# HGRN layer: VectorE's and ScalarE's instruction orders written by hand beside TensorE's, with weight splits and projection finishes at fixed places

## The chip, the cores and the metric

The kernel runs on one core of one Trainium2 chip. Its time is the device time of one execution in microseconds (us), and lower is better. Three executions of the kernel before were timed; a profiled execution of the same program gives the trace that is read below.

Five engines matter: TensorE (PE; its weight loads are shown apart as PEld), VectorE (DVE), ScalarE (ACT), GpSimd (POOL) and SyncE (SP), which issues the DMAs. Each takes its own instructions in their order, and semaphores tie the engines together.

## The reference: what is computed

A trunk of two layers over 512 tokens of width 1024, in float32. Each layer has a token mixer, a squared-ReLU MLP and a gated embedding, with a layer norm after mixer and MLP. Layer 0 mixes with Mamba-2 SSD, layer 1 with HGRN2, and the change touches the HGRN2 mixer alone:

```python
q, fz, v, g = jnp.split(u @ w_in, 4, axis=-1)
log_f = jnp.logaddexp(jnp.log(lb), jnp.log1p(-lb) + jax.nn.log_sigmoid(fz))
k = (1.0 - lb) * jax.nn.sigmoid(-fz)
...
b_cs = jnp.cumsum(chunked(log_f, k_dim), axis=2)
...
def step(s_prev, inp):
    q_, kk, v_, b_ = inp
    diff = b_[:, :, None] - b_[:, None, :]
    dec = jnp.exp(jnp.where(mask, diff, -jnp.inf))
    scores = jnp.einsum('blhk,bshk,blshk->bhls', q_, kk, dec)
    o = jnp.einsum('bhls,bshv->blhv', scores, v_) + jnp.einsum('blhk,bhkv->blhv', q_ * jnp.exp(b_), s_prev)
    b_last = b_[:, -1]
    s_new = jnp.exp(b_last)[..., None] * s_prev + jnp.einsum(
        'bshk,bshv->bhkv', kk * jnp.exp(b_last[:, None] - b_), v_)
    return s_new, o
...
o = rms_norm(o, norm_w).reshape(bsz, seq, D_MODEL) * jax.nn.silu(g.astype(jnp.float32))
return o.astype(u.dtype) @ w_out
```

There are 8 heads of 128 channels. A score between two tokens carries, for each of the 128 channels, the product of the forget gates between them.

## The kernel before, in words

**Products in float32.** A weight tile of 128x1024 comes by one DMA into a raw tile (three of them). A *split* makes two tiles of it: ACT casts it to the high part (`whi`, L113) and DVE subtracts that from the raw tile to get the low part (`wlo`, L115). Every product is then three matmuls (`mm3`, L119 to L121): high x high, high x low, low x high. Six buffers hold high parts and six low parts.

**The HGRN stage** has two strands that share TensorE.

The *background* computes projections that need no head's result: query and forget gate of a head (`qf`, two tiles, 16 `mm3`), values and gates of two heads (`vg`, four tiles), and the first half of the output projection (`out0`). They run in the order `q0 q1`, then `JOBS`: q2 q3 q4 q5 v2 q6 q7 v3 o (the values of heads 0 to 3 are computed ahead of the stage). A projection's *finish* empties its PSUM banks: for `qf` a copy (L880), a table load, a sigmoid (L882), a scaling (L883), a second sigmoid (L885) and a scaling (L886) on ACT; for `vg` four bank copies (L863) and a Silu over two tiles (L865).

The *core* (`hcore`) takes the heads in pairs: 0/1, 2/3, 4/5, 6/7. Scores within 32 tokens are built in levels m = 0 to 4. At the first, third and fifth level (m = 0, 2, 4) TensorE multiplies keys by queries for each block of 32 tokens (L981: 88, 56 and 16 columns), into one PSUM bank per head. DVE then multiplies keys and queries by decays (L987, L992) and the decays among themselves (L1000), once a level, and copies the scores out of the bank through masks (L962). `distant` (L955, L956) makes the queries of the next wide level. After the levels come blocks farther apart (L1046), transposes of the keys (L1077), state sums (L1089, L1093), outputs (L1107, L1109), a norm with the gate (L1114 to L1119) and transposes of the result (L1127), which ACT and DVE split (L1128, L1129). `enter_heads` (L935) prepares the next pair.

**What sets the order.** `hcore` is a generator: at each `yield n` the caller lets the background run for about n us of matmuls (`fill`), so TensorE's order is written out by hand (`manual_schedule` with TensorE alone). FILL, STEPS, AHEAD and LAST hold those amounts; for heads 6 and 7 they are scaled by 0.78. On VectorE, ScalarE and the DMA queue a scheduler orders the instructions by priority. In `unit` a split has a raised priority (LEAD = 100) and is placed as the scheduler sees fit; the finish of a projection is recorded directly behind its last matmul; `issue_after` ties `enter_heads` to a state copy (L1091).

The PSUM buffers: four banks for projections (`pj`), two for the cores' scores and outputs (`py0`, `py1`, one per head of the pair), one for transposes (`pt`), one for sums (`pm`). A new tile of a tag with one buffer waits until the last reader of the old one is done: the third level's matmuls wait for the masked copies of the first.

## Time and profile before

| what | value |
|---|---|
| runs timed | 1424.92, 1425.13, 1426.7 us (median 1425.13) |
| profiled execution, its own time | 1426.6 us |
| its span, first to last instruction | 1424.8 us |
| TensorE's granted clock over the span | 1.00 |
| VectorE / ScalarE busy in the stretch 820 to 1020 us | 142.3 / 115.9 us of 200 |
| HBM traffic over the span | 124 GB/s |

The profile is one execution of the program, taken by the hardware profiler. A row of the view in order of time has the start in us, the duration in us, the engine, the line of the kernel, the operation, "out<-in" with the tiles' names, the shapes, how many alike follow each other (x), and in brackets the idle time of the engine before it with what ended that. A row of the view by groups has the busy time, the mean duration in ns and the idle time before. TensorE's rows overlap, since matmuls are pipelined and their ends are modelled; its pace is read from the starts. Line numbers are those of the kernel before; after the change they are higher (old L962, L987, L1128 are new L1014, L1037, L1184).

### The profile page before, as it was taken

What the parts mean: (1) busy time and instruction counts of PE and PEld (TensorE: products, weight loads), DVE (VectorE), ACT (ScalarE), POOL (GpSimd) and SP (SyncE); (2) the same over time, 40 slices, a digit from 0 to 9 for tenths busy, and PEclk for the clock granted to TensorE, in tenths of its full rate; (3) what the DMA queues carried; (4) which work ended last, traced back from release to release, by engine and by line L of the source; (5) the groups of instructions that cost most, each with busy time, mean ns of one, the idle gap of its engine ahead of it and who ended that gap; (6) DMA issues with size and microseconds to landing.
All of it is one profiled execution on the core that took longest, in us unless ns stands there. A gap on an engine that the chain in (4) does not pass through costs nothing.

```text
span 1424.8 us, 20421 instructions
## 1 busy us (share of the span) xinstructions
PE 1413.6 (99%) x8061; PEld 1174.6 (82%) x8061; DVE 1057.4 (74%) x1760; ACT 754.5 (53%) x1134; POOL 1.8 (0%) x12
## 2 busy tenths in 40 slices
PE   9999999999999999999999999999999999999998
PEld 7888888888888888888888887887898888888887
DVE  7988687787967667677986576678685867667873
ACT  6776454563265454545545547655555454544641
POOL 0000000000000000000000000000000000000000
PEclk9999999999999999999999999999999999999999
DMA  8432323333433444444621321222163444444231
GB/s 298 142 130 92 119 89 119 104 107 126 152 119 121 158 130 153 133 148 163 215 82 49 133 90 60 75 90 90 50 232 104 148 137 145 148 133 163 89 118 45
DMA packets 49392, 178.02 MB, mean 125 GB/s; under 512 B 5521, under 2 KB 6289, under 8 KB 49169
## 3 DMA queue, kind: packets, MB, share of 16 engines
q1 hardware_dynamic: 49296, 176.73, 36.8%
q8 instruction: 63, 1.03, 0.3%
q14 instruction: 33, 0.26, 0.1%
HBM read 174.54 MB, written 2.16 MB: 124 GB/s over the span
## 4 chain that ended last, share of the span: by engine, by line
PE 94%; DVE 3%; ACT 2%; DMA 1%; issue 0%; SPq 0%; ACTq 0%; DVEq 0%
PE pj L119 23%; PE pj L120 23%; PE pj L121 23%; PE py L119 5%; PE py L121 5%; PE py L120 5%; PE py L735 1%; PE py L741 1%; PE py L981 1%; PE pm L705 1%; DVE wlo L115 1%; PE pt L233 1%; PE pt L693 1%; DMA r<-in_w 1%; PE py L1107 0%
## 5 line engine op out<-in xcount | busy, mean ns | idle before, releaser
L113 ACT CAST whi<-raw 128x1024 fp32r<-128x1024 f32 x222 | 233.0, 1052 | 330.3 <-PE pj L120 234.1
L119 PE MATMUL pj<-b,whi 128*128 128x512 f32 (+1 forms) x1006 | 382.1, 381 | 0.7 <-ACT b L237 0.7
L120 PE MATMUL pj<-b,whi 128*128 128x512 f32 (+1 forms) x1006 | 380.6, 379 | 1.0 <-DVE b L238 1.0
L121 PE MATMUL pj<-b,wlo 128*128 128x512 f32 (+1 forms) x1006 | 379.2, 377 | 0.0
L115 DVE TENSOR_TENSOR wlo<-raw,whi 128x1024 fp32r<-128x1024 f32 x222 | 269.8, 1220 | 142.2 <-ACT whi L113 136.8
L120 PEld LDWEIGHTS pj<-b,whi 128*128 128x128 f32 x1006 | 189.4, 188 | 34.2 <-DVE b L238 1.2
L119 PEld LDWEIGHTS pj<-b,whi 128*128 128x128 f32 x1006 | 188.9, 188 | 34.1 <-ACT b L237 0.9
L121 PEld LDWEIGHTS pj<-b,wlo 128*128 128x128 f32 x1006 | 189.2, 188 | 33.6
L121 PE MATMUL pj<-whi,b 128*128 128x512 f32 x544 | 212.8, 392 | 0.0
L119 PE MATMUL pj<-whi,b 128*128 128x512 f32 x536 | 212.7, 397 | 0.0
L120 PE MATMUL pj<-wlo,b 128*128 128x512 f32 x536 | 210.2, 393 | 0.0
L121 PEld LDWEIGHTS pj<-whi,b 128*128 128x128 f32 x544 | 102.1, 188 | 20.9
L119 PEld LDWEIGHTS pj<-whi,b 128*128 128x128 f32 x536 | 100.7, 188 | 20.6 <-ACT b L1128 0.6
L120 PEld LDWEIGHTS pj<-wlo,b 128*128 128x128 f32 x536 | 100.8, 188 | 19.4
L113 ACT CAST whi<-r 128x1024 fp32r<-128x1024 f32 x72 | 75.7, 1053 | 67.8 <-PE pj L121 38.6
L115 DVE TENSOR_TENSOR wlo<-r,whi 128x1024 fp32r<-128x1024 f32 x72 | 87.6, 1219 | 23.8 <-ACT whi L113 23.2
L121 PE MATMUL py<-whi,b 128*128 128x512 f32 (+1 forms) x250 | 96.9, 388 | 0.0
L120 PE MATMUL py<-wlo,b 128*128 128x512 f32 x224 | 87.2, 389 | 0.0
L119 PE MATMUL py<-whi,b 128*128 128x512 f32 x224 | 87.1, 390 | 0.0
L121 PEld LDWEIGHTS py<-whi,b 128*128 128x128 f32 x250 | 46.9, 188 | 9.7
L634 DVE SCALAR_TENSOR_TENSOR cv<-pj,cst,cv 128x509 f32<-128x509 f32 (+2 forms) x66 | 48.7, 744 | 3.6 <-ACT cv L631 2.8
L119 PEld LDWEIGHTS py<-whi,b 128*128 128x128 f32 x224 | 42.1, 188 | 9.1 <-DVE sg L494 0.3
(303 smaller groups left out, 1864.7 us busy)
## 6 DMA issues: line engine op xcount, KB each, us to landing
raw<-in_w SPq DMA_DIRECT2D x112, 512.0 KB, 3.3
r<-in_w SPq DMA_DIRECT2D x64, 512.0 KB, 3.4
raw<-in_wssd SPq DMA_DIRECT2D x36, 512.0 KB, 3.4
a<-csd SPq DMA_DIRECT2D x16, 512.0 KB, 3.6
raw<-in_wso SPq DMA_DIRECT2D x16, 512.0 KB, 3.3
raw<-in_wg SPq DMA_DIRECT2D x16, 512.0 KB, 3.4
raw<-in_whq SPq DMA_DIRECT2D x16, 512.0 KB, 3.3
raw<-in_whvg SPq DMA_DIRECT2D x14, 512.0 KB, 3.2
```

What stands on the lines that cost most here:

```text
L113: nc.scalar.copy(hi[:, :n], f)
L115: nc.vector.tensor_sub(lo[:, :n], f, f32(hi[:, :n]))
L119: nc.tensor.matmul(out, sh, mh, start=start, stop=False, **kw)
L120: nc.tensor.matmul(out, sh, ml, start=False, stop=False, **kw)
L121: nc.tensor.matmul(out, sl, mh, start=False, stop=stop, **kw)
L233: nc.tensor.transpose(pt[:, j * P : (j + 1) * P], src[:, k * P : (k + 1) * P], ident)
L634: nc.vector.scalar_tensor_tensor(cv[:, d:], ps[:, : T - d], convw[:, i, k : k + 1], cv[:, d:], ALU.mult, ALU.add)
L693: nc.tensor.transpose(pt[:, c * P : (c + 1) * P], xs[:, c * P : (c + 1) * P], ident)
L705: nc.tensor.matmul(pst_[:, c * P : (c + 1) * P], btok[:, c, :], xw[:, c].rearrange("p h q -> p (h q)"), start=True, stop=True)
L735: nc.tensor.matmul(yd[64 * r : 64 * r + 64, sl], xdt[:, 2 * c + r, :], m[:, r, sl], start=True, stop=True)
L741: nc.tensor.matmul(yo[:, c * P : (c + 1) * P], pv[:, c - 1].rearrange("p h q -> p (h q)"), cm[:, c * P : (c + 1) * P], start=True, stop=True,)
L981: nc.tensor.matmul(pcs[r][bs, at : at + n], kk[r][:, ts], qs, start=True, stop=True)
```

## The change

ScalarE and VectorE join `manual_schedule`: their instructions in the HGRN stage now stand in the order in which the source records them. What was left to the scheduler gets a place:

- **Loads and splits.** All weight tiles are listed ahead (`sources`). `lift` issues the next load; `feed` splits one raw tile if fewer than READY = 4 split tiles wait, and lifts another; `take` hands the background the oldest split tile. `feed` stands at the end of the levels' stages, after the state sums and after each transposition of results.
- **Finishes.** `qf` and `vg` put their finish into a list (`due`), and `flush` carries it out: at each stage's end, when the next `qf` begins (all but one), when `vg` takes its third bank, before `out0`, and when a core needs the result.
- **The core.** `distant` of the third level is recorded one level earlier, and the first and third levels' masked copies one level later, behind the products of the second and fourth. `enter_heads` runs `distant` of the first level, and is no longer tied to a state copy.

The core of the diff:

```diff
+READY = 4
+    def flush(n=0):
+        while len(due) > n:
+            due.pop(0)()
+    def feed(n=1):
+        while n and raised and len(ready) < READY:
+            ready.append(split(raised.pop(0), 0))
+            lift()
+            n -= 1
+    def take():
+        if not ready:
+            feed()
+        u = ready.pop(0)
+        if not cores:
+            feed()
+        return u
...
-                units.append(unit(a["whvg"][4 * i + j]))
+                units.append(take())
             if j == 0:
+                if c == 2:
+                    flush()
                 pss[c] = bank(psj, "pj")
...
     def qf(h):
+        flush(1)
...
-            hi, lo = unit(a["whq"][2 * h + w])
+            hi, lo = take()
...
+        due.append(finish)
...
             if m in wide:
                 pcs = [py(r) for r in R]
-                for r in R:
-                    distant(r, half)
...
-            for r in R:
+            if m == 1:
+                for r in R:
+                    distant(near[r], qd[r], tot[r], 4)
+            for r in R if m not in wide else ():
                 sc, scb, pc = scs[r], scbs[r], pcs[r]
-                if m in wide:
-                    n = 88 - wide[m]
-                    u = half
+                if m < 4:
+                    w = m - 1
+                    n = 88 - wide[w]
+                    u = 1 << w
...
             if m not in wide:
+                flush()
+                feed()
                 yield FILL[0] * STEPS[m // 2]
...
         if h0 < 6:
-            for r in R:
-                need("qf", h0 + 2 + r)
-            with tc.issue_after(carried.ins):
-                enter_heads(h0 + 2)
+            enter_heads(h0 + 2)
+        feed()
...
             nc.vector.scalar_tensor_tensor(s.l(i0 + r), pt, hnw[:, 0:1], f32(s.h(i0 + r)), ALU.mult, ALU.subtract)
+            if r:
+                flush()
+            feed()
             yield FILL[4]
...
-    with tc.manual_schedule(engines={mybir.EngineType.PE}):
+    with tc.manual_schedule(engines={mybir.EngineType.PE, mybir.EngineType.Activation, mybir.EngineType.DVE}):
+        for _ in range(RAWS):
+            lift()
+        feed(READY)
...
-                need("qf", 1)
+                enter_heads(0)
```

The orders of the two built programs stand side by side like this. TensorE's is the same in the whole stage up to the outputs of heads 6 and 7. SP's differs by two loads of `who` that stand two places later. ACT and DVE differ in most of the stage; this is the changed program between heads 0/1 and 2/3 (new line numbers, buffer numbers left out):

```
ACT  L1184 b <- pt            last transposes of heads 0/1
     L921  xs <- pj           finish of projection 4 (flush)
     L923  table load, sz <- pj
     L924  sz <- sz
     L926  cv <- pj
     L927  cv <- cv
     L114  whi <- raw         cast of one split (feed)
DVE  L1185 b <- pt, b
     L116  wlo <- raw, whi    subtraction of the same split
     L1037 L1042 L1050        products of level 1, heads 2 and 3
     L1037 L1042 L1050        products of level 2
     L986 L986 L987           distant, both heads
     L1014 x5, L1014 x5       masked copies of level 1, head by head
```

And on ACT in the pair 4/5, after the fourth and fifth levels:

```
ACT  L1044 L1044              half of the queries copied
     L114  whi <- raw
     L1086 x8                 diagonal blocks copied
     L921 .. L927             finish of projection 7
     L114  whi <- raw x2
```

TensorE's order in that place: L1031 (fifth level), three matmuls into the second value bank, then the third value bank.

More of the change, by code (lines that the diff above doesn't have):

```diff
@@ L841, in trunk, with lift @@
     nc.vector.tensor_scalar(lbc, lb, -1.0, 1.0, ALU.mult, ALU.add)
+    sources = []
+    raised, ready, cores = [], [], []
+    def lift():
+        if sources:
+            raw = mk(raws, [P, 1024], "raw")
+            with tc.high_priority(offset=LEAD):
+                nc.sync.dma_start(raw, sources.pop(0))
+            raised.append(raw)
+    due = []
+    def flush(n=0):
[13 more added lines that the diff above has]
+        return u
     def vg(i):
@@ L863, in vg, with finish @@
                 nc.scalar.copy(res[c // 2][:, c % 2], pss[c])
-        for r in res:
-            nc.scalar.activation(r[:, :, 256:], r[:, :, 256:], AF.Silu)
-        made["vg", i] = res
+        def finish():
+            for r in res:
+                nc.scalar.activation(r[:, :, 256:], r[:, :, 256:], AF.Silu)
+            made["vg", i] = res
+        due.append(finish)
     def qf(h):
+        flush(1)
         ps = []
         for w in range(2):
-            hi, lo = unit(a["whq"][2 * h + w])
+            hi, lo = take()
             ps.append(bank(psj, "pj"))
@@ L876, in qf, with finish @@
                 yield 0.65
-            if w == 0:
-                q = tmp("xs", [P, T])
-                nc.scalar.copy(q, ps[0])
-        f = tmp("sz", [P, T])
-        nc.scalar.activation(f, ps[1], AF.Sigmoid)
-        nc.scalar.activation(f, f, AF.Identity, scale=lbc[:, h : h + 1], bias=lb[:, h : h + 1])
-        kk = tmp("cv", [P, T])
-        nc.scalar.activation(kk, ps[1], AF.Sigmoid, scale=-1.0)
-        nc.scalar.activation(kk, kk, AF.Copy, scale=lbc[:, h : h + 1])
-        made["qf", h] = q, f, kk
+        def finish():
+            q = tmp("xs", [P, T])
+            nc.scalar.copy(q, ps[0])
+            f = tmp("sz", [P, T])
+            nc.scalar.activation(f, ps[1], AF.Sigmoid)
+            nc.scalar.activation(f, f, AF.Identity, scale=lbc[:, h : h + 1], bias=lb[:, h : h + 1])
+            kk = tmp("cv", [P, T])
+            nc.scalar.activation(kk, ps[1], AF.Sigmoid, scale=-1.0)
+            nc.scalar.activation(kk, kk, AF.Copy, scale=lbc[:, h : h + 1])
+            made["qf", h] = q, f, kk
+        due.append(finish)
     def out0():
+        flush()
         for h in range(2):
-            units = [unit(a["who"][2 * h + i]) for i in range(2)]
+            units = [take() for i in range(2)]
             for c in range(NCH):
@@ L901, in out0 @@
                 nc.vector.scalar_tensor_tensor(d, d, ALPHA, ps, ALU.mult, ALU.add)
+    for job in ["q0", "q1"] + JOBS:
+        name, n = {"v": ("whvg", 4), "q": ("whq", 2), "o": ("who", 4)}[job[0]]
+        sources += [a[name][n * int(job[1:] or 0) + j] for j in range(n)]
     def background():
@@ L913, in need @@
         while key not in made:
-            next(bg)
+            if due:
+                flush()
+            else:
+                next(bg)
         return made[key]
@@ L926, in blocks32, with distant @@
         return t.rearrange("p (b u) -> p b u", u=32)
+    def distant(near, qd, tot, u):
+        sv = qd.rearrange("p k (s f u) -> p k s f u", f=4, u=u)
+        tv = tot.rearrange("p (k s f) -> p k s f", k=T // 32, f=4)
+        v2 = near[:, :, 64:80].rearrange("p k (s t u) -> p k s t u", t=2, u=u)
+        v3 = near[:, :, 80:].rearrange("p k (s u) -> p k s u", u=u)
+        for t in range(2):
+            nc.vector.tensor_mul(v2[:, :, :, t], sv[:, :, :, 2 + t], bc(tv[:, :, :, 1 + t], 3, u))
+        nc.vector.tensor_mul(v3, v2[:, :, :, 1], bc(tv[:, :, :, 1], 3, u))
     def enter_heads(h0):
@@ L935, in enter_heads @@
             nc.vector.tensor_mul(qd[r], blocks32(q[r]), blocks32(f[r]))
+            distant(near[r], qd[r], f[r], 1)
+        for r in R:
             nc.scalar.copy(near[r][:, :, :32], blocks32(q[r]))
@@ L941, in hcore @@
         R = range(2)
-        if h0 == 0:
-            enter_heads(0)
+        cores.append(h0)
         q, f, kk, near, qd = made.pop(("core", h0))
@@ L946, in hcore @@
         tokens = lambda c, b: (slice(b, b + 32), slice(c * P + b, c * P + b + 32))
-        def distant(r, u):
-            sv = qd[r].rearrange("p k (s f u) -> p k s f u", f=4, u=u)
-            tv = tot[r].rearrange("p (k s f) -> p k s f", k=T // 32, f=4)
-            v2 = near[r][:, :, 64:80].rearrange("p k (s t u) -> p k s t u", t=2, u=u)
-            v3 = near[r][:, :, 80:].rearrange("p k (s u) -> p k s u", u=u)
-            for t in range(2):
-                nc.vector.tensor_mul(v2[:, :, :, t], sv[:, :, :, 2 + t], bc(tv[:, :, :, 1 + t], 3, u))
-            nc.vector.tensor_mul(v3, v2[:, :, :, 1], bc(tv[:, :, :, 1], 3, u))
         tot = f
@@ L1009, in hcore @@
                     nc.vector.tensor_mul(far[r][:, :, 2], far[r][:, :, 1], bc(tv[:, :, 1], 2, 32))
-            for r in R:
+            if m == 1:
+                for r in R:
+                    distant(near[r], qd[r], tot[r], 4)
+            for r in R if m not in wide else ():
                 sc, scb, pc = scs[r], scbs[r], pcs[r]
-                if m in wide:
-                    n = 88 - wide[m]
-                    u = half
+                if m < 4:
+                    w = m - 1
+                    n = 88 - wide[w]
+                    u = 1 << w
                     pc = pc[:, : n * NCH].rearrange("p (c l) -> p c l", c=NCH)
-                    if m == 0:
+                    if w == 0:
                         keep(scb, lmask[:, 0], pc[:, :, :32])
-                    pc = pc[:, :, 32 - wide[m] :]
-                    m0 = 1 + 3 * (m // 2)
+                    pc = pc[:, :, 32 - wide[w] :]
+                    m0 = 1 + 3 * (w // 2)
                     keep(scb, lmask[:, m0], pc[:, :, :32])
@@ L1033, in hcore @@
             if m not in wide:
+                flush()
+                feed()
                 yield FILL[0] * STEPS[m // 2]
@@ L1069, in settle @@
                     nc.scalar.copy(scs[r][32 * k : 32 * k + 32, odd::2, 32 * (k + 1) :], pc)
+        flush()
+        feed()
         yield FILL[0] * STEPS[3]
@@ L1090, in hcore @@
             sv.append(tmp("pv", [P, 3, P]))
-            carried = nc.scalar.copy(sv[r][:, 0], pss[:, 0:P])
+            nc.scalar.copy(sv[r][:, 0], pss[:, 0:P])
             for c in range(1, 3):
@@ L1129, in hcore @@
             nc.vector.scalar_tensor_tensor(s.l(i0 + r), pt, hnw[:, 0:1], f32(s.h(i0 + r)), ALU.mult, ALU.subtract)
+            if r:
+                flush()
+            feed()
             yield FILL[4]
     halves = []
-    with tc.manual_schedule(engines={mybir.EngineType.PE}):
+    with tc.manual_schedule(engines={mybir.EngineType.PE, mybir.EngineType.Activation, mybir.EngineType.DVE}):
+        for _ in range(RAWS):
+            lift()
+        feed(READY)
         for h in range(0, 8, 2):
@@ L1144, in trunk @@
             pass
+        flush()
     h_s, *after = norm(2)
```

## The prediction

> **What bounds the kernel now.** First the page's busy times: TensorE (PE) fills the whole span, so the time is its own work plus what it waits.

> ```profile
> span 1424.8 us, 20421 instructions
> PE 1413.6 (99%) x8061; PEld 1174.6 (82%) x8061; DVE 1057.4 (74%) x1760; ACT 754.5 (53%) x1134; POOL 1.8 (0%) x12
> ```

> VectorE (DVE) and ScalarE (ACT) have room, so the number of their instructions does not matter; when they run does. Second, TensorE's rows in order of time through the HGRN stage (about 808 to 1020 us), first one at its normal pace, then every long wait:

> ```profile
> 942.09 0.39 PE L119 MATMUL pj<-whi,b 128*128 128x512 f32 x1
> 942.32 0.39 PE L120 MATMUL pj<-wlo,b 128*128 128x512 f32 x1
> ...
> 863.40 0.55 PE L1077 MATMUL pt<-cst,cv 128*128 128x128 f32 x3 [1.39 <-ACT btok L1079]
> ...
> 925.92 0.55 PE L1127 MATMUL pt<-cst,cbm 128*128 128x128 f32 x3 [0.47 <-DVE b L1129]
> ...
> 972.99 0.66 PE L1127 MATMUL pt<-cst,cbm 128*128 128x128 f32 x4 [1.02 <-DVE b L1129]
> ...
> 983.16 0.45 PE L981 MATMUL py<-qd,cv 128*32 128x56 f32 x19 [0.42 <-DVE qd L956]
> ```

> A matmul is shown as 0.39 us but the next starts 0.23 later, so a bracket leaves out 0.16. The four waits are 1.55, 0.63, 1.18 and 0.58, together 3.9 us. **That is all the change can win here**: 0.3%. It does not shorten TensorE's work, whose order stays the same through this stage.

> **The change, part by part.** The order of the built program now follows the source on ACT and DVE. Three things move against TensorE's fixed order: the masked copies out of the scores' PSUM bank (old L962) of the first level come after all products of the second; each weight split (ACT cast, DVE subtraction) has a fixed place, and DVE stops there until the cast is done; a projection's finish (old L880 to L886) runs on ACT at its flush. For a removed stall I ask which of these is late next.

> *DVE between the first and third level.* The third level's matmuls reuse the bank, so they wait for the first level's copies. Before, for heads 2 and 3:

> ```profile
> 882.73 1.42 PE L981 MATMUL py<-qd,cv 128*32 128x88 f32 x64
> 890.43 0.99 PE L981 MATMUL py<-qd,cv 128*32 128x56 f32 x64
> ...
> 883.62 0.42 DVE L987 TENSOR_TENSOR cv<-cv,sz 128x256 f32<-128x256 f32 x1 [2.07 <-PE py L981]
> 883.96 0.42 DVE L992 TENSOR_TENSOR qd<-qd,sz 128x256 f32<-128x256 f32 x1
> 884.29 0.30 DVE L962 COPY_PREDICATED scb<-lmask,py 128x128 f32<-128x128 uint8 x1
> ...
> 885.16 1.47 DVE L962 COPY_PREDICATED scb<-lmask,py 128x128 f32<-128x128 uint8 x8
> 886.38 0.50 DVE L987 TENSOR_TENSOR cv<-cv,y 128x256 f32<-128x256 f32 x1
> ...
> 888.94 1.21 DVE L115 TENSOR_TENSOR wlo<-raw,whi 128x1024 fp32r<-128x1024 f32 x1
> 890.08 0.28 DVE L956 TENSOR_TENSOR qd<-qd,y 128x128 f32<-128x128 f32 x1
> ...
> 821.26 0.42 DVE L1000 TENSOR_TENSOR y<-sz 128x256 f32<-128x256 f32 x1
> ...
> 822.19 0.29 DVE L1000 TENSOR_TENSOR y<-y 128x128 f32<-128x128 f32 x1
> ...
> 832.83 0.17 DVE L1052 TENSOR_TENSOR y<-y 128x4 f32<-128x4 f32 x1
> 833.03 0.17 DVE L1053 TENSOR_TENSOR y<-y 128x4 f32<-128x4 f32 x1
> ```

> From 883.62 to 890.36 are 6.74 us; without the split (1.14 to the next start) 5.6 are this pair's own. Added: the products of decays (L1000), done early before (821 and 822) and now in source order: each starts 0.08 before its forerunner ends, so 0.34 + 0.21 a head, 1.1. The ten copies took 0.2 + 1.2 + 0.1 = 1.5 while two heads alternated; now five in a row write one tile, and a step that needs the one before starts 0.03 after its end (832.83 to 833.03), so three of five cost 0.33 and two 0.10: 1.2 a head, 0.9 more. With 0.2 for products that now depend on each other, **the chain is 7.8 us** (6.7 if copies overlap as before, 8.2 if each hand-over costs more). The first head's copies end 1.2 earlier.

> *Heads 0 and 1.*

> ```profile
> 835.82 0.43 DVE L987 TENSOR_TENSOR cv<-cv,sz 128x256 f32<-128x256 f32 x1 [0.73 <-PE py L981]
> ...
> 842.63 0.99 PE L981 MATMUL py<-qd,cv 128*32 128x56 f32 x64
> ```

> The chain ends at 843.6; the second head's half of the group is due 0.45 after 842.63. Wait 0.5 (0 to 1.3).

> *Heads 2 and 3.* ACT, after the last transposes of heads 0 and 1, now has the finish of projection 4 and a cast ahead of it, and DVE's subtraction for that cast stands in front of the whole chain:

> ```profile
> 879.08 0.58 ACT L880 COPY xs<-pj 128x512 f32<-128x512 f32 x1
> 880.08 0.69 ACT L1128 ACTIVATE b<-pt,cst 128x512 fp32r<-128x512 f32 x1 [0.41 <-PE pt L1127]
> 885.55 1.06 ACT L113 CAST whi<-raw 128x1024 fp32r<-128x1024 f32 x1 [4.78 <-PE pj L120]
> 886.62 1.28 ACT L882 ACT_TABLE_LOAD   x1
> 887.92 0.60 ACT L882 ACTIVATE sz<-pj 128x512 f32<-128x512 f32 x1
> ...
> 889.59 0.72 ACT L886 ACTIVATE cv<-cv,lbc 128x512 f32<-128x512 f32 x1
> ```

> 880.77 (end of L1128) + 0.58 (L880) + 3.69 (table load through L886, 886.62 to 890.31) + 1.06 (cast) = 886.1; + 1.14 (subtraction) = 887.2; + 7.8 = 895.0 for the second head, 893.8 for the first. TensorE is there at 890.43: 3.4, then 0.45 of its own, then 0.75. Wait 4.2 (3.1 to 5.4). The split's weights are not needed yet; it is the queue behind them that TensorE wants.

> [...]

> *Heads 4 and 5.* The same, with the values' gate in place of the finish:

> ```profile
> L865 ACT ACTIVATE b<-b 128x512 f32<-128x512 f32 x2 | 1.3, 650 | 0.0
> ```

> 1.28 + 2 x 0.64 = 2.6 against 4.3: 1.7 less. Wait 2.5 (1.4 to 3.3).

> *The same pair, a PSUM bank.* Projection 7's finish is now flushed when the third value bank is taken. On ACT it stands behind the eight copies of the diagonal blocks; before it ran ahead of them:

> ```profile
> 943.02 0.59 ACT L882 ACTIVATE sz<-pj 128x512 f32<-128x512 f32 x1
> ...
> 947.42 2.46 ACT L1032 COPY sc<-scb 32x128 f32<-32x128 f32 x8 [2.02 <-DVE scb L962]
> ...
> 947.17 0.35 DVE L962 COPY_PREDICATED scb<-lmask,py 128x64 f32<-128x64 uint8 x2
> ...
> 944.22 0.74 PE L981 MATMUL py<-xs,cv 128*32 128x16 f32 x64
> ...
> 945.69 0.39 PE L119 MATMUL pj<-whi,b 128*128 128x512 f32 x1
> ```

> DVE is done at 947.5 + 0.3 (two more decay products); + 2.5 + 0.6 (L880, which frees the bank) = 950.9. TensorE wants it after this level's group and three matmuls, 945.7: 5.2, and 0.5 more at the next bank (three activations, 1.9, against six matmuls, 1.4). Wait 5.7 (5 to 6).

> *Heads 6 and 7.* The background is scaled by 0.78, so less covers DVE:

> ```profile
> 976.33 0.89 PE L981 MATMUL py<-qd,cv 128*32 128x88 f32 x36
> ...
> 989.37 0.74 PE L981 MATMUL py<-xs,cv 128*32 128x16 f32 x64
> ...
> L901 DVE SCALAR_TENSOR_TENSOR acc<-acc,pj 128x512 f32<-128x512 f32 x8 | 5.4, 684 | 1.9 <-PE pj L121 1.9
> ```

> Third level due 6.25 after 976.33 (983.16 less 0.58). DVE: start 0.9 after it, chain to the first head's copies 6.6, and a split of the out projection, 1.14: 8.6. Wait 2.4, then 0.75: 3.1 (2 to 3.8). Fifth level due 6.2 later: two updates of acc 1.2, eight products 2.7, decays 0.6, copies 0.75, two splits 2.3, from 0.45 on: 8.0. Wait 1.8 and 0.4: 2.2 (1.4 to 3).

> *The rest.* Later splits stand before the last heads' state sums: 1 (0 to 2). Gone: 863.40, 925.92 and 972.99, where copy and subtraction now come first, 3.4. Moved DVE and ACT work off these places costs nothing: it lies under TensorE's matmuls. The loads' order on SP changes by two entries and the raw tiles stay full.

> **Sum.** 0.5 + 4.2 + 2.5 + 5.7 + 3.1 + 2.2 + 1.0 - 3.4 = +15.8. The profiled execution took 1426.6 (span 1424.8 and 1.8 around it): 1442.4. The median of the runs, 1425.13, is 1.5 lower: **1441**. Low ends give +9.5 (1435), high ends +21.4 (1446.5).

> **Rivals.** *TensorE loses its pace in the long waits.* At the start it ran at half pace:

> ```profile
> 5.88 1.06 PE L583 MATMUL pj<-b,whi 128*128 128x512 f32 x2
> ```

> Two matmuls of 512 columns in 1.06 less the 0.39 overhang are 0.43 apart or so, against 0.23 later; that lasted from 1.45 to about 8 us. If a wait of 3.4 or 5.2 does it again, each costs half of 6.6: +3.3 to +6.6, 1444 to 1448. Against it: no wait before is over 1.6 us, so no row shows it. [...]

> *Waits feed each other.* While TensorE waits, DVE and ACT catch up, and later waits shrink. If fifth level and half the bank's wait go so: 1436; with heads 4 and 5 too, 1431 to 1434.

> *Faster: the cover holds.* At heads 2 and 3 the point is that finish, cast, subtraction and chain fit between 880.08 and 890.43. They would if ACT reached the finish early and DVE kept its chain at 6.7 or below; then new waits vanish and the four old ones too: 1425.1 - 3.9 = 1421.2. For it: ACT is busy 53%. Against: ACT's order puts L1128, which waits for TensorE, ahead of the finish, and 10.4 us must hold about 15.

> **Numbers.** Forecast (1436 to 1446.5) 0.62; pace lost 0.16; waits shrink (1429 to 1436) 0.10; partly covered, within 0.2% (2.9 us, about what a measurement here can tell) 0.06; faster 0.06. Slower 0.88, same 0.06, faster 0.06. Leaving out both ends, the range is 1431 to 1448.

> **What would show it.** In the changed profile TensorE's waits should name DVE's masked copies at the third-level matmuls of all four pairs (longest at heads 2 and 3), one ACT activation at a value matmul near 950 us, and no wait for btok near 863. DVE should stand 4 to 5 us before a subtraction at the entry of heads 2 and 3, waiting for its cast. If DVE's chain there is near 6 us, or no third-level matmul waits, I am wrong; half-pace matmuls after a wait show the first rival.

## The result, and the profile after

The changed kernel takes 1446.14 us (median of 4 runs, 1444.66 to 1446.52) against 1425.03 for the kernel before beside it: a ratio of 1.0143, 95% interval 1.013 to 1.0156. It is 21.1 us slower. That is inside the range, 5 above the forecast, and at the place of the first rival. The profiled execution took 1446.26 (span 1444.5). Of the version below with VectorE given back to the scheduler, the profiled execution ran at a granted clock of 0.65 throughout (2022.55 us): it is left out of the times, and its rows are not read.

The page of the changed kernel: TensorE's busy time rose by 6.2 us, though it does the same 8061 matmuls, and the span by 19.7.

```profile
span 1444.5 us, 20408 instructions
PE 1419.8 (98%) x8061; PEld 1179.1 (82%) x8061; DVE 1062.5 (74%) x1760; ACT 755.0 (52%) x1134; POOL 1.9 (0%) x12
```

What TensorE waited for: the two long rows of the list over the whole span (total, times, longest; each leaves out 0.16 as before). The two names are the forecast's: masked copies (L1014, the old L962) and one ACT activation (L921, the old L880). The stage has no btok wait left, and one more of 0.5 behind it (L1165, for `pv`).

```profile
PE py L1031 <- DVE scb L1014: 12.1, 9, 3.6
PE pj L120 <- ACT xs L921: 5.1, 1, 5.1
```

The entry of heads 2/3, in order of time, first ACT and DVE, then TensorE:

```profile
878.79 1.28 ACT L923 ACT_TABLE_LOAD   x1
...
882.68 1.03 ACT L114 CAST whi<-raw 128x1024 fp32r<-128x1024 f32 x1
```

```profile
883.75 1.22 DVE L116 TENSOR_TENSOR wlo<-raw,whi 128x1024 fp32r<-128x1024 f32 x1 [4.66 <-ACT whi L114]
884.89 0.42 DVE L1037 TENSOR_TENSOR cv<-cv,sz 128x256 f32<-128x256 f32 x1
...
890.11 2.71 DVE L1014 COPY_PREDICATED scb<-lmask,py 128x128 f32<-128x128 uint8 x10
```

```profile
887.65 0.39 PE L122 MATMUL pj<-whi,b 128*128 128x512 f32 x1
891.68 0.60 PE L1031 MATMUL py<-qd,cv 128*32 128x56 f32 x32 [3.65 <-DVE scb L1014]
892.97 0.97 PE L1031 MATMUL py<-qd,cv 128*32 128x56 f32 x32 [0.68 <-DVE scb L1014]
893.87 0.80 PE L120 MATMUL pj<-whi,b 128*128 128x512 f32 x1
894.47 0.63 PE L121 MATMUL pj<-wlo,b 128*128 128x512 f32 x1
...
898.73 0.56 PE L122 MATMUL pj<-whi,b 128*128 128x512 f32 x1
899.13 0.40 PE L120 MATMUL pj<-whi,b 128*128 128x512 f32 x1
```

Read from the left: ACT runs the finish, then the cast; DVE stands 4.66 us before the subtraction; its chain then takes 884.89 to 892.82, 7.9 us; TensorE, done at 887.9, waits for it. And then what the forecast left to a rival: the next matmuls start 0.43 apart instead of 0.23, until 899.1. The bank wait in pair 4/5 looks the same, ACT's rows first:

```profile
954.76 2.44 ACT L1086 COPY sc<-scb 32x128 f32<-32x128 f32 x8 [6.77 <-DVE scb L1014]
957.23 0.58 ACT L921 COPY xs<-pj 128x512 f32<-128x512 f32 x1
```

```profile
952.38 0.40 PE L122 MATMUL pj<-whi,b 128*128 128x512 f32 x1
957.87 0.80 PE L120 MATMUL pj<-whi,b 128*128 128x512 f32 x1 [5.09 <-ACT xs L921]
958.46 0.63 PE L121 MATMUL pj<-wlo,b 128*128 128x512 f32 x1
...
963.98 0.39 PE L122 MATMUL pj<-whi,b 128*128 128x512 f32 x1
```

At heads 6/7 the pace holds behind the third level, and falls behind the fifth:

```profile
998.88 0.60 PE L1031 MATMUL py<-qd,cv 128*32 128x56 f32 x32 [2.30 <-DVE scb L1014]
1000.16 0.60 PE L1031 MATMUL py<-qd,cv 128*32 128x56 f32 x32 [0.69 <-DVE scb L1014]
...
1007.20 0.45 PE L1031 MATMUL py<-xs,cv 128*32 128x16 f32 x32 [1.45 <-DVE scb L1014]
1007.95 0.44 PE L1031 MATMUL py<-xs,cv 128*32 128x16 f32 x32 [0.31 <-DVE scb L1014]
1008.33 0.80 PE L120 MATMUL pj<-whi,b 128*128 128x512 f32 x1
...
1011.83 0.40 PE L122 MATMUL pj<-whi,b 128*128 128x512 f32 x1
```

The same in stretches of 20 us (stretch, length, busy us of PE, PEld, DVE, ACT, POOL with instructions, then the granted clock of TensorE, DMA share, GB/s); from 990 to 1030 the clock is 0.96, and in every other stretch from 870 on it is 1.00:

```profile
890.00:910.00 20.00, 17.63 (x275) 14.06 (x276) 11.56 (x45) 5.36 (x13) 0.00 (x0) 0.83 0.09 29
...
950.00:970.00 20.00, 14.91 (x206) 11.52 (x205) 9.38 (x29) 7.34 (x15) 0.00 (x0) 0.83 0.21 70
```

TensorE's order is the same in both kernels up to the end of the stage, so its n-th matmul in one trace can be set against the n-th in the other. The wait is the gap between two starts less the usual gap:

| place (us, after) | predicted | measured |
|---|---|---|
| third level, heads 0/1 (842.5) | 0.5 | 0.9 |
| third level, heads 2/3 (891.7, 893.0) | 4.2 | 4.6 |
| third level, heads 4/5 (942.9, 944.2) | 2.5 | 2.6 |
| bank, pair 4/5 (957.9) | 5.7 | 5.3 |
| third level, heads 6/7 (998.9, 1000.2) | 3.1 | 3.2 |
| fifth level, heads 6/7 (1007.2, 1008.0) | 2.2 | 2.0 |
| behind (1024.5) | 1.0 | 0.7 |
| old stalls gone | -3.4 | -4.0 |
| half pace, three stretches | none | 2.8 + 2.9 + 1.4 |

The waits sum to 19.3 against 19.2 forecast. Waits less old stalls are +15.3, the half pace is +7.1: 22.4. Over the stage the trace has 22.0; the spans differ by 2.3 less, because in this execution the half pace of the start ended sooner (full pace from about 5 us instead of 7.6, 1.3 us saved), and because a stall of 1.0 in the MLP behind (1047.74 in the trace of before) is not in this one. The change touches neither place.

### The profile page after: what moved, and what is told of

It reads as the page before. It is cut to its first block, busy times and chain, and to the rows that moved or that the text cites. A ratio compares the mean times of both kernels' runs of the same rounds, so it can differ in the third digit from the quotient of the medians.

```text
span 1444.5 us, 20408 instructions
## 1 busy us (share of the span) xinstructions
PE 1419.8 (98%) x8061; PEld 1179.1 (82%) x8061; DVE 1062.5 (74%) x1760; ACT 755.0 (52%) x1134; POOL 1.9 (0%) x12
## 4 chain that ended last, share of the span: by engine, by line
PE 93%; DVE 4%; ACT 2%; issue 1%; DVEq 0%; ACTq 0%
PE pj L120 24%; PE pj L121 23%; PE pj L122 23%; PE py L120 5%; PE py L122 5%; PE py L121 5%; PE py L736 1%; PE pt L234 1%; PE py L742 1%; DVE scb L1014 1%; PE pm L706 1%; DVE wlo L116 1%; PE pt L694 1%; DVE cv L1037 0%; PE py L1163 0%
## 5 line engine op out<-in xcount | busy, mean ns | idle before, releaser
L114 ACT CAST whi<-raw 128x1024 fp32r<-128x1024 f32 x222 | 232.5, 1050 | 292.3 <-PE pj L121 203.5
L120 PE MATMUL pj<-b,whi 128*128 128x512 f32 (+1 forms) x1006 | 382.0, 381 | 0.7 <-ACT b L238 0.7
L121 PE MATMUL pj<-b,whi 128*128 128x512 f32 (+1 forms) x1006 | 380.5, 378 | 0.0
L120 PE MATMUL pj<-whi,b 128*128 128x512 f32 x536 | 216.1, 403 | 5.1 <-ACT xs L921 5.1
L120 PEld LDWEIGHTS pj<-b,whi 128*128 128x128 f32 x1006 | 188.9, 188 | 34.4 <-ACT b L238 0.9
L121 PEld LDWEIGHTS pj<-b,whi 128*128 128x128 f32 x1006 | 189.4, 188 | 33.2 <-issue 0.9
L122 PE MATMUL pj<-whi,b 128*128 128x512 f32 x544 | 215.2, 396 | 0.0
L121 PE MATMUL pj<-wlo,b 128*128 128x512 f32 x536 | 213.2, 398 | 0.0
L120 PEld LDWEIGHTS pj<-whi,b 128*128 128x128 f32 x536 | 102.4, 191 | 26.9 <-ACT xs L921 5.5
L122 PEld LDWEIGHTS pj<-whi,b 128*128 128x128 f32 x544 | 103.8, 191 | 21.4
L121 PEld LDWEIGHTS pj<-wlo,b 128*128 128x128 f32 x536 | 102.6, 191 | 19.9
L121 PE MATMUL py<-wlo,b 128*128 128x512 f32 x224 | 87.2, 389 | 0.0
L120 PE MATMUL py<-whi,b 128*128 128x512 f32 x224 | 87.1, 390 | 0.0
L120 PEld LDWEIGHTS py<-whi,b 128*128 128x128 f32 x224 | 42.0, 188 | 9.1 <-DVE sg L495 0.3
```

Of the source, the lines that this page charges most:

```text
L114: nc.scalar.copy(hi[:, :n], f)
L120: nc.tensor.matmul(out, sh, mh, start=start, stop=False, **kw)
L121: nc.tensor.matmul(out, sh, ml, start=False, stop=False, **kw)
L122: nc.tensor.matmul(out, sl, mh, start=False, stop=stop, **kw)
```

## The experiments

**Theory:** two orders by hand meet: ACT's puts finish and diagonal copies ahead of what DVE or TensorE wants next; DVE's puts a subtraction and slow copies ahead of the third level; behind a long wait (3.7 and 5.3 us here) TensorE loses half its pace (matmuls 0.43 us apart for 0.23). **Rivals:** the waits feed each other, so that undoing one moves it on; or the half pace has another cause.

### Three edits, alone and together

*The split ahead of the finish* at the end of each pair:

```diff
+            feed()
             if r:
                 flush()
-            feed()
             yield FILL[4]
```

> At the end of each pair of heads the weight split now stands ahead of the projection's finish; nothing else differs from the changed kernel (1446.1 us). Theory (the split's subtraction waits for a cast that stands behind the finish): the first third-level wait of heads 2/3 falls from 3.7 to at most 0.5 us and that of heads 4/5 from 1.7 to at most 0.5, the second head's 0.9 stays at both, and TensorE's half pace from 893.9 to 899.1 goes with the long wait (2.9 us). 3.7 + 1.7 + 2.9 less up to 1.0 is 7.3 to 8.3 us: 1438 to 1439. Rival 1 (the half pace is not caused by the wait): 4.4 to 5.4, about 1441, with the window 890 to 910 still at a granted clock near 0.83. Rival 2 (the waits feed each other): the finish, now later, makes TensorE wait elsewhere, 1443 or more.

Measured: 1438.46 us (ratio to before 1.0087, 1.0072 to 1.0102), 7.7 less than the changed kernel. DVE's brackets at the entry shrink from 4.66 to this:

```profile
880.75 1.22 DVE L116 TENSOR_TENSOR wlo<-raw,whi 128x1024 fp32r<-128x1024 f32 x1 [0.18 <-ACT whi L114]
882.64 0.43 DVE L1037 TENSOR_TENSOR cv<-cv,sz 128x256 f32<-128x256 f32 x1 [0.66 <-PE py L1031]
```

The chain now waits for TensorE, not for ACT. The first third-level waits of heads 2/3 and 4/5 are gone (3.7 and 1.7), and the clock in 890 to 910 is 1.00. The theory holds; both rivals fall here. At heads 6/7 the stretch of half pace now stands behind the third level (993.1 to 996.5) instead of the fifth.

*The copies of the two heads in turn*: the same five steps, each for both heads before the next step.

```diff
-            for r in R if m not in wide else ():
-                ...
-                    keep(scb, lmask[:, m0], pc[:, :, :32])
+                for r in R:
+                    keep(scbs[r], lmask[:, m0], at[r][:, :, :32])
...
+                for t in range(2):
+                    for r in R:
+                        keep(sv[r][:, :, :, 2 + t], mv[:, m0 + 1, :, 2 + t], v2[r][:, :, :, t])
```

> The masked copies of the first and second level (line 1014) alternate between the two heads, as the scheduler had them before, instead of five in a row on one tile; same place, same number. Theory (a copy that writes the tile of the copy before it starts only at its end): ten copies take 1.5 us instead of 2.7, the second head's own wait at the third level (0.9 at each of four pairs) and at the fifth level of heads 6/7 (0.5) goes, the first head's changes by 0.2 at most: 3 to 4 us less, 1442 to 1443. Rival (a copy from PSUM takes its 0.3 us whatever stands beside it): the ten still take 2.7, the first head waits 1.2 longer and the second about none: 1446 to 1448.

Measured: 1440.94 us (1.0104, 1.0089 to 1.0119), 5.2 less. The ten copies of heads 2/3:

```profile
889.95 1.83 DVE L1014 COPY_PREDICATED scb<-lmask,py 128x128 f32<-128x128 uint8 x10
```

1.83 against 2.71: five in a row on one tile do cost, as the prediction had it, 0.9 a pair. The second head's own wait is gone at all four pairs; the first waits 0.26 more. It brought more than expected because the fifth level of heads 6/7 no longer waits (2.0; 1.4 of it comes back at the products between blocks), and the half pace behind it went as well (1.4).

*The finish at the second value bank* instead of the third:

```diff
-                if c == 2:
+                if c == 1:
                     flush()
```

> A value projection asks for the pending finish at its second bank instead of its third, so that projection 7's finish stands ahead of the eight copies of the diagonal blocks on ScalarE. Theory: the bank wait of 5.3 us at 957.87 and the half pace behind it (2.9) go, 8.2 us: 1438. Rival 1 (the half pace is not caused by the wait): 5.3, 1441. Rival 2 (the waits feed each other: VectorE is late there as well): half of it comes back as a wait for VectorE's copies or products at the fifth level or behind it: 1441 to 1444, with a new wait of 2 us or more in the same pair.

Measured: 1439.5 us (1.0089, 1.0072 to 1.0106), 6.6 less. The list of waits has no row for L921 any more, and the clock in 950 to 970 is 1.00. So 5.3 and 2.9 went, and no wait came back in pair 4/5. 1.6 less was won than these 8.2: in this run half pace stands behind both places of heads 6/7, as short stretches (clock 0.83 in 990 to 1010), where the changed kernel has it behind the fifth level alone.

*All three:*

> The three edits together: split ahead of the finish, copies in turn, finish at the second bank. Theory (the waits are apart from each other and the half pace comes from the long ones alone): 3.7 + 1.7 + 5.3 + 4.0 of waits and 7.2 of half pace go, less up to 1.0: about 21 less, 1424 to 1427, near the kernel before (1425.0), with a granted clock of 1.00 in every window. What is left is 2 to 3 us at the third and 1.5 to 2 at the fifth level of heads 6/7. Rival 1 (half pace not caused by waits): 1432. Rival 2 (waits feed each other): 1435 or more.

Measured: 1427.46 us (1.0012, 1.0002 to 1.0021), 18.7 less and 0.5 above the expected range. What the three won alone adds up to 19.5: the waits hardly feed each other. Of the stage's waits there remain:

```profile
PE py L1031 <- DVE scb L1014: 3.1, 4, 2.6
...
PE py L1106 <- DVE scb L1014: 1.3, 1, 1.3
```

The granted clock was not 1.00 everywhere, as I had expected: behind the 2.6 at heads 6/7 it was 0.50 for 3.4 us (982.1 to 985.5; 0.91 in 970 to 990).

### Whose order costs what

One engine at a time was given back to the scheduler, with the changed source (`engines` of `manual_schedule` is the whole edit).

> The changed kernel with VectorE's order given back to the scheduler; TensorE's and ScalarE's stay by hand and the source is the same. Theory (VectorE's fixed order makes the waits at the third and fifth levels, ScalarE's the bank wait): of 12.7 us of waits for the masked copies 2 or less stay, the half pace at 893.9 and 1008.3 goes with them (4.3), the bank wait and its half pace stay (8.2), and the two old stalls for VectorE's subtraction (1.8) come back: 1446.1 - 10.7 - 4.3 + 1.8 = 1433, 1431 to 1434. Rival (the cast's late place on ScalarE alone makes the entry late, whoever orders VectorE): heads 2/3 still wait 3 us or more with half pace behind, 1438 or more.

Measured with VectorE given back: 1430.04 us (1.003, 1.002 to 1.0039). 1 better than the theory's range, 8 away from the rival. Which waits stayed is not shown by rows of its own.

> The changed kernel with ScalarE's order given back to the scheduler; TensorE's and VectorE's stay by hand. Theory: the bank wait and its half pace go (8.2), the cast is no longer behind the finish, so the waits at the entry of heads 2/3 and 4/5 fall as in the run with the split first (7.7, half pace with them), and an old stall or two for ScalarE's copies comes back (1 to 2.5): 1430 to 1433. What stays is VectorE's: 0.9 and the like at each third level, 2 to 3 at both places of heads 6/7. Rival (VectorE's fixed order alone holds heads 2/3): a wait of 3 us or more there, 1437 or more.

Measured with ScalarE given back: 1435.41 us (1.0075, 1.0061 to 1.0089), 2.4 above the expected range. Its waits show why:

```profile
PE py L1031 <- DVE scb L1014: 5.8, 7, 1.4
PE pt L1135 <- ACT btok L1137: 2.2, 2, 2.0
PE pt L1183 <- DVE b L1185: 1.7, 2, 1.0
```

The bank wait and the long one at heads 2/3 are gone, but the old stalls (btok, b) are back in full, not one or two of them: it was ScalarE's order that had removed all three. Half pace stands here as well, behind the fifth level of heads 6/7 (996.8 to 1000.2; 0.91 in 990 to 1010).

> The changed source, but only TensorE's order by hand, as before: the scheduler orders VectorE and ScalarE. Theory (the time is lost by the fixed orders, not by where the source now puts splits, finishes, copies and decays): 1424 to 1428, the old stalls back, no wait over 1.7 us in the stage and a granted clock of 1.00. Rival (the moved copies and the splits' fixed places cost by themselves, through priorities or buffers): 1430 or more.

Measured with both given back: 1427.6 us (1.0012, 1.0003 to 1.0021). The source as changed costs 1.8 us when the scheduler orders it; 18.5 of the 21 us are the two fixed orders. In its trace the old stall for btok is 1.0 longer (2.6 instead of 1.6). That trace is of its fastest execution (1426.07), so where the rest of the 1.8 lies is not shown.

### What is left of DVE's chain

On top of the three edits, the decays of the first two levels are made in `enter_heads`:

```diff
+        tots = [tmp("y", [P, T]) for r in R]
+        for m in range(2):
+            for r in R:
+                ...
+                nc.vector.tensor_mul(tots[r][:, at : at + nb], tv[:, :, 0], tv[:, :, 1])
...
-                nc.vector.tensor_mul(nt[r], tv[:, :, 0], tv[:, :, 1])
+                if m > 1:
+                    nc.vector.tensor_mul(nt[r], tv[:, :, 0], tv[:, :, 1])
```

> The run with the three edits (1427.5 us), and besides the products of decays of the first two levels (line 1050) are made when the heads are entered, so that 1.1 us of them leave VectorE's chain ahead of the third level. Theory (that chain is the only thing late there): the 0.8 left at the third level of the first three pairs goes, the 2.6 of heads 6/7 falls to 1.5: 3 us less, 1424 to 1425, and the short half pace behind 982.9 (1.5) may go as well (1423). Rival (the same work is in the way at the entry instead): 1426 to 1428, with a wait at the state sums or the transposes behind the entry.

Measured: 1424.54 us (0.9993, 0.9984 to 1.0002). 2.9 less, near the theory; the waits left at the first three pairs (0.35 each in the run before, not the 0.8 that I had put down) are gone, the one of heads 6/7 fell from 2.7 to 1.65, and with it went the half pace: the clock is 1.00 in every stretch of the stage. The 1.1 us that the prediction charged to the decays' place is the 1.1 that heads 6/7 gained.

Next, the full background for the last pair (`LAST = 1.0`):

> The run with early decays (1424.5 us), and the last pair of heads gets the full share of background matmuls instead of 0.78 of it. Theory (what is left at heads 6/7 is VectorE's chain against too little cover): 1.3 us more cover at the third level, 0.9 at the fifth; the waits of 1.65 and 1.44 there fall to about 0.3 and 0.5, and 0.5 to 1.5 of it comes back at the state sums and score products behind, where the background has run out: 1423 to 1424. Rival (the background's work is fixed, so all of it comes back): 1424.5 to 1425.5.

Measured: 1422.12 us (0.9972, 0.9961 to 0.9983), 2.4 less, more than expected: of the waits at heads 6/7 0.3 is left, and only 0.8 and 0.6 came back behind.

And VectorE to the scheduler, ScalarE by hand with the first and third edit:

> VectorE's order by the scheduler, TensorE's and ScalarE's by hand, and two of the three edits: split ahead of the finish, finish at the second bank. Theory (in the run with VectorE scheduled, 1430.0 us, what is lost against the kernel before is the bank wait and the half pace behind it): 5.3 + 2.9 go, and up to 1 at the entries: 1421 to 1422, faster than before (1425.75), with a granted clock of 1.00 throughout and no wait in the stage over 1.5 us. Rival (ScalarE's fixed order costs elsewhere too, or the bank wait returns as another): 1424 or more.

Measured: 1422.3 us (0.9973, 0.9962 to 0.9983), near the theory and clear of the rival; clock 1.00 throughout, and in the stage only these waits:

```profile
PE py L1165 <- DVE pv L1151: 0.5, 1, 0.5
PE py L1031 <- DVE scb L1014: 0.4, 1, 0.4
```

Two versions, one with VectorE by hand and one without, beat the kernel before by the same 0.27%. That is close to what all four old stalls together are worth (3.9 us). In the first, 2.4 of it came with the background's share; no run gave that share to the kernel before, so what it is worth there is not shown.

### Is it idleness that halves the pace?

Seven pauses were put into the version with the full background:

```diff
+        def pause(n):
+            pt = bank(pst, "pt")
+            nc.tensor.transpose(pt[:, :P], ident, ident)
+            t = mk(sm, [P, 32], "pause")
+            for _ in range(n):
+                nc.scalar.copy(t, pt[:, :32])
+            nc.tensor.transpose(pt[:32, P : 2 * P], t, ident)
```

> The run with the full share, with seven pauses for TensorE: one small transposition, 2 to 14 small copies on ScalarE in a row, one small transposition that reads the last copy. They change nothing of the results and stand behind the cross-block scores and at the end of the pairs. What is wanted is the pace of the matmuls behind each pause against its length (2 to 6 us). Theory (idleness by itself brings the half pace): matmuls 0.43 us apart instead of 0.23 behind the pauses of 4 us and more and none behind those under 2; the slow stretch lasts about 6 us and costs about 3 whatever the length of the pause: 1423 + 24 of pauses + 3 to 5 times 2.5, 1452 to 1460. Rival 1 (the loss grows with the wait: twice as much behind 6 us as behind 3.5). Rival 2 (not idleness but what VectorE and ScalarE do at the old places slows TensorE): no half pace behind any pause, about 1447.

Measured: 1448.24 us (one run). Six pauses held TensorE, for 17.2 us in all (1.4, 3.8, 2.0, 2.6, 3.3 and 4.3), less than I had planned. Half pace came behind 3.8, 3.3 and 4.3, none behind the other three, so the rival without half pace falls, and a pause shorter than the 4 us expected is enough. By the granted clock it lasted 3.41 us behind the first two and 6.83 behind the 4.3, of which 1.6 lay in the pause itself. Set against the run with the full background matmul by matmul, it cost 1.6, 1.6 and 2.1 us, less than expected; that and the shorter pauses make the lower time. Whether the loss doubles behind 6 us is open: no pause was that long. The one behind 3.3:

```profile
963.75 0.27 PE L1020 MATMUL pt<-cst 128*128 128x128 f32 x1
967.12 0.29 PE L1024 MATMUL pt<-cst,pause 128*32 128x128 f32 x1 [3.09 <-ACT pause L1023]
...
968.31 0.43 PE L123 MATMUL pj<-whi,b 128*128 128x512 f32 x1
968.54 0.63 PE L121 MATMUL pj<-whi,b 128*128 128x512 f32 x1
...
972.07 0.40 PE L122 MATMUL pj<-wlo,b 128*128 128x512 f32 x1
```

It sets in 1.4 us after TensorE had taken up work again at full pace. The reverse: in the changed kernel, matmuls whose result nobody reads fill part of the two long waits.

```diff
+    def busy(n):
+        ps = bank(psm, "pm")
+        for _ in range(n):
+            nc.tensor.matmul(ps, x_s.h(0, slice(0, P)), x_s.h(0), start=True, stop=True)
...
+                    if i == 3:
+                        busy(16)
...
+                if (h0, m) == (2, 2):
+                    busy(12)
```

> The changed kernel (1446.1 us) with 28 matmuls of 512 columns more, whose result nobody reads: 12 ahead of the third level of heads 2/3, where TensorE waits 3.7 us, and 16 ahead of the third value bank, where it waits 5.3. They fill 2.7 and 3.6 us of these waits and end none of them. Theory (TensorE loses its pace because it is idle): the half pace at 893.9 and 957.9 goes, 5.8 us: 1440.4, though TensorE does more. Rival (what it waits for slows it, or the loss is in what comes behind the wait whatever TensorE did meanwhile): 1446 or more.

Measured: 1443.84 us (1.0133, 1.0116 to 1.015): 2.3 less than the changed kernel (1446.14), not 5.8. The bank wait in its trace, and heads 6/7's third level:

```profile
955.75 0.50 PE L120 MATMUL pj<-whi,b 128*128 128x512 f32 x1 [1.44 <-ACT xs L928]
956.08 0.40 PE L121 MATMUL pj<-wlo,b 128*128 128x512 f32 x1
```

```profile
994.41 0.68 PE L1040 MATMUL py<-qd,cv 128*32 128x56 f32 x32 [2.30 <-DVE scb L1021]
995.70 0.97 PE L1040 MATMUL py<-qd,cv 128*32 128x56 f32 x32 [0.61 <-DVE scb L1021]
996.60 0.80 PE L120 MATMUL pj<-whi,b 128*128 128x512 f32 x1
997.19 0.63 PE L121 MATMUL pj<-wlo,b 128*128 128x512 f32 x1
...
1001.46 0.47 PE L122 MATMUL pj<-whi,b 128*128 128x512 f32 x1
```

Both old stretches are at full pace (clock 1.00 in 890 to 910 and 950 to 970), with more work and the same instructions to wait for. But the wait of 2.5 at heads 6/7, behind which the changed kernel kept its pace, now has half pace behind it (994.8 to 1001.6), and that behind the fifth level is gone. Set against the changed kernel matmul by matmul, 2.8 and 2.3 us are won at the two filled waits, 2.6 lost at heads 6/7 and 1.5 won behind the fifth level: about 4 by the trace; 2.3 by the medians. So in these runs it is idleness, and which stretch of 3.41 us it falls in (an estimate, see the last section).

## Why the prediction was right, and where it was wrong

- **TensorE's own time bounds the kernel, and DVE and ACT matter by their order.** Right. ACT and DVE do the same work in the versions read, from 1422 to 1446 us (DVE busy 1057 to 1063 us, ACT 754 to 756).
- **DVE's chain, 7.8 us.** Measured 7.9. Both of its new terms are shown by experiment: copies in a row (0.9; measured 0.9) and decays in source order (1.1; measured 1.1).
- **Heads 2/3: finish, cast, subtraction, chain; 4.2.** Measured 4.6; the split ahead of the finish removes the first head's 3.7. **Heads 4/5,** 2.5: 2.6, the same order.
- **The bank, 5.7.** Measured 5.3, and removed by the earlier finish. The 0.5 at the next bank did not come: by then the matmuls before it ran at half pace. In the run with filled waits, where they ran at full pace, 0.3 of it came (957.6).
- **Heads 6/7, 3.1 and 2.2.** 3.2 and 2.0. That too little background covers DVE there is shown by the full share.
- **Gone, 3.4.** Right in size (4.0 with the fourth stall, which the sum should have taken off as well). I credited copy and subtraction "first" in both orders; given back, ScalarE alone brings all three stalls back.
- **The rival "waits feed each other".** Fell: 19.5 apart, 18.7 together.
- **The failed step** is the argument against the first rival, "no wait before is over 1.6 us, so no row shows it", and with it the 0.16. The kernel before could not show it, having no long wait; my own sum, with waits of 4.2 and 5.7, said that the changed one would. The size per stretch (3.3) was near the 2.8 and 2.9; the third stretch, behind waits of 1.5 and 0.5, was not on my list. Forecast and this rival came true together: 1441 is 5 too low, all of it and more the half pace of 7.1. Without it the same waits give 1439; that 1446.1 still lies inside the range, 0.4 below its end, is luck, since the range has no term for the half pace. And the 0.43 between matmuls does not follow from 1.06 less 0.39, as the rival has it, though it is the measured step.

## What to carry to other kernels

When an order is written out by hand, each instruction in an engine's queue waits for all that stands before it (here DVE's chain behind a subtraction that was held for 4.66 us): put what another engine waits for (a cast, a copy that frees a bank) ahead of what is only due later (a finish), and alternate steps that write one tile (ten copies took 1.83 us for 2.71). Fix only the engine whose order gains something: here ScalarE's removed the stalls, and VectorE could as well be left to the scheduler. Where TensorE bounds the kernel, price a wait at its length and, where about 2 us of idleness can fall within 3.4 us, at 1.4 to 2.9 us of half pace behind it, as here.

## What the hardware showed that I had not expected

```profile
994.66:998.07 3.41, 1.91 (x9) 1.26 (x7) 3.31 (x13) 0.00 (x0) 0.00 (x0) 1.00 0.18 35
998.07:1001.48 3.41, 1.92 (x67) 1.64 (x68) 3.27 (x12) 0.00 (x0) 0.00 (x0) 1.00 0.31 124
1004.90:1008.31 3.41, 1.65 (x68) 1.13 (x66) 3.34 (x10) 0.58 (x1) 0.00 (x0) 1.00 0.48 150
1008.31:1011.72 3.41, 3.41 (x19) 2.75 (x9) 3.34 (x12) 0.00 (x0) 0.00 (x0) 0.50 0.52 162
```

```profile
989.72:993.13 3.41, 1.06 (x64) 0.96 (x64) 3.20 (x13) 0.00 (x0) 0.00 (x0) 1.00 0.42 154
993.13:996.54 3.41, 3.41 (x19) 2.67 (x9) 3.41 (x12) 0.81 (x2) 0.00 (x0) 0.50 0.02 5
```

In the changed kernel the edge at 998.07 cuts the wait in two, and TensorE is busy 1.91 and 1.92 us on its two sides; in the other run the wait lies in one window, which is left with 1.06. In the window from 1004.90 TensorE was busy for 1.65 us, and the pace fell behind it. Counted over the thirteen traces that are read, each on its own grid and with 0.16 added to a bracket (an estimate, since the ends of matmuls are modelled), of the windows entered at full pace all 12 with more than 2.1 us of idleness lost it (3.0 and 3.4 in the changed kernel), none with less than 1.8 did (1.7 on either side of 998.07), and of the six between 1.87 and 2.08 four did (2.08 from 1004.90). In the changed kernel the full pace came back each time at the end of the first window without a wait in it (busy for all of its 3.41 us; the first two stretches also hold a window with the rest of the wait, busy for 2.73 and 2.66). That the bound is near 2 us of 3.4 is read from these places; no run varied it by itself.
